# Two-layer hybrid encoder: token-on-partition projections in 512-column blocks, two token tiles at a time

## The chip, the cores and the metric

The kernel runs on one core of a Trainium2 chip. The metric is the device time of one execution in microseconds, as the median of a few runs. Everything is computed in fp32; large matmuls are done in three passes on operands that are split into two exact parts (called hi and lo below).

## What is computed

The reference is a trunk of two layers over 512 tokens of 1024 features. Each layer is a mixer and a convolutional FFN, each wrapped as x += RMSNorm(f(RMSNorm(x))).

```python
def _ssd_mlstm_mixer(h, w_in, ...):          # layer 0
    z, xbc, dt_raw, q, k, v, o_pre, gates = _split(h @ w_in, L0_SPLITS)
    xbc = jax.nn.silu(_dwconv(xbc, conv_w, conv_b))
...
    y = _head_rmsnorm(y.reshape(bsz, s, SSD_D_INNER) * jax.nn.silu(z), ssd_norm, SSD_GROUPS)
...
    hm = jax.nn.sigmoid(o_pre) * hm.reshape(bsz, s, MLSTM_D)
    hm = _head_rmsnorm(hm, mlstm_norm, MLSTM_HEADS)
    return jnp.concatenate([y, hm], axis=-1) @ w_out

def _gla_mixer(h, w_in, ...):                # layer 1
    q, k, v, r, g_lr = _split(h @ w_in, L1_SPLITS)
...
    o = _head_rmsnorm(o.reshape(bsz, s, GLA_DV), gla_norm, GLA_HEADS) * jax.nn.silu(r)
    return o @ w_out
```

The projections z, v, o_pre (layer 0) and v, r (layer 1), each 1024 columns wide, are wanted with tokens on the partitions. The others (k, q, xbc, the small gates, all of the FFN and the output projections) are wanted with features on the partitions.

## The kernel before

**Projections.** Work comes in two forms. A `Job` (line 259) is one 128-row tile of W^T h: eight k steps of three matmuls, 512 tokens wide, 24 matmuls into one PSUM bank, with the weight as the stationary operand. `nat_job` (line 344) is the other form, h^T W: 256 weight columns, for each of the four tiles of 128 tokens 24 matmuls that are 256 columns wide, with h as the stationary operand. In the profile's names a Job's matmul is `pj<-s,hi` and a nat_job's is `pj<-hi,s` or `pj<-lo,s`; all of them carry the line of a recording helper (L105), so the rows are told apart by tile names.

**PSUM.** The eight banks are split into tags (line 1356): `pj` has two, used by the streams' projections, `ps` and `pm` have three each, used by the scans. A nat_job takes one `pj` bank per token tile, so the two banks alternate: while one is filled, the other is read out by `post`, which runs on ScalarE. For z and r (lines 684 and 1123) `post` is silu in the form z(1 + tanh(z/2)): ScalarE reads the bank once with Identity and the token's scale into SBUF, then takes tanh from SBUF, and VectorE multiplies. For layer 0's v and o (lines 868 and 873) it is two reads of 128 columns each, into two heads; for layer 1's v one read. A Job's `post` starts with a VectorE read of the bank (`s<-pj,srow`).

**Weights.** They stream from HBM in 234 slabs of 1024 columns. `w_prep` (line 222) loads a slab, casts it to its hi part on ScalarE and takes the rest (lo) on VectorE. Five hi/lo buffers exist (`W_SPLIT`), and a slab is prepared four ahead of the one in use. A Job uses one slab, a nat_job two, for all four token tiles.

**Order.** The mixers weave generators by estimated engine time (`weave`, line 47). In layer 0 stream A is the projections, in the order p0 x0 z0 p1 x1 z1 p2 p3 (line 1341): a "p" is four Jobs (k, q) and two nat_jobs (v, o), an "x" is three or six Jobs, a "z" two nat_jobs; after them come eight Jobs of the first output projection. Stream B is the gate rows and the SSD scan, stream C the mLSTM heads. In layer 1 stream A is five Jobs and eight nat_jobs (four v, four r), and two streams run two GLA heads each; head n waits for the marks `v{n}` and `r{n}`. The framework then schedules by this order as priority and by its own estimate of when an instruction is ready; on the chip each engine runs its queue strictly in the order that came out. Work tiles of 512 columns get one of 64 slots, planned from the traced order; tiles of 256 columns come from a pool of six.

Of the kernel before, what the change touches and what calls it, by code (L numbers as in the profile page):

```python
# [30 lines left out]
# columns of the constant block  # L31
# [9 lines left out]
class _Balance:  # L41
    """Work issued so far to TensorE and VectorE, in ns, to weave two streams evenly."""
# [4 lines left out]
    def weave(self, streams, done):  # L47
        """streams: (generator, engine whose work it is paced by, total ns of that work, head start in ns).
        The stream least far along goes on, if what it needs is done."""
        st = [{"g": g, "e": e, "n": float(n), "t": -lead / float(n), "need": None} for g, e, n, lead in streams]  # L50
        while st:
            ok = [x for x in st if x["need"] is None or x["need"] in done]
            assert ok, [x["need"] for x in st]
            x = min(ok, key=lambda x: x["t"])
            t0 = getattr(self, x["e"])
            try:
                x["need"] = next(x["g"])
            except StopIteration:
                st.remove(x)
            x["t"] += (getattr(self, x["e"]) - t0) / x["n"]  # L60


class _Life:
    """First and last use of every work tile, in program order, and from that a slot for each."""
# [16 lines left out]
    def plan(self, slots):  # L81
        """The slot that has been free for longest."""
        until, res = [-1] * slots, []
        for a, z in zip(self.first, self.last):
            i = min(range(slots), key=lambda j: until[j])
            assert until[i] < a or until[i] < 0, "too few slots"
            until[i] = z + 1
            res.append(i)
        return res


class _Eng:
    """An engine that notes which tiles its instructions touch and how long they take."""
# [37 lines left out]
def kernel(ctx: ExitStack, tc: tile.TileContext, xin, wst, cst, dsk, gw2, out, life=None, plan=None):  # L131
# [104 lines left out]
    def w_take(n, width=P):  # L236
        """The next n tiles of `width` columns of the stream, as (hi, lo) pairs."""
        res = []
        for _ in range(n):
            c0 = wstate["unit"]  # L240
            i, o = divmod(c0, 1024)
            while len(wstate["ready"]) < i + 1 + W_AHEAD and wstate["next"] < NSLAB:
                w_prep()
            hi, lo = wstate["ready"][i]
            res.append((hi[:, o:o + width], lo[:, o:o + width]))
            wstate["unit"] += width
        return res

    def mm3(o, a, b, first, last):
        """o += a^T b with operands in two exact parts."""  # L250
        (ah, al), (bh, bl) = a, b
        PE.matmul(o, ah, bh, start=first, stop=False)
        PE.matmul(o, ah, bl, start=False, stop=False)
        PE.matmul(o, al, bh, start=False, stop=last)
# [4 lines left out]
    class Job:  # L259
        """One 128-row tile of W^T h."""  # L260
# [38 lines left out]
    def run_group(jobs, r, mid=None, serial=False):  # L299
        """Several jobs together, one k tile after the other (or one job after the other)."""  # L300
# [43 lines left out]
    def nat_job(h, post, hi=False):  # L344
        """256 columns of h^T W with tokens on the partitions."""
        w = w_take(KD, 256)
        for c in range(NCH):
            o = pj()
            for k in range(KD):
                hh, hl = h[k]  # L350
                tk = slice(c * P, (c + 1) * P)
                mm3(o[:, :256], (hh[:, tk], hl[:, tk]), w[k], k == 0, k == KD - 1)
            with hp(hi):
                post(o[:, :256], c)
            yield

# [4 lines left out]
    def col_sum(o, i, acc):  # L361
        """o[tok, 2i + t]: the sum of acc[:, tok] over the partitions, for two tiles of tokens."""
        for t in range(2):
            PE.matmul(o[:, 2 * i + t:2 * i + t + 1], acc[:, t * P:(t + 1) * P], ones[:, 0:1], start=True, stop=True)

    def rstd(v, rs):
        """rs = 1 / sqrt(v / D + eps) for columns v."""
        S.activation(rs, v, AF.Sqrt, bias=eps1, scale=1.0 / D)
        V.reciprocal(rs, rs)

    def spread(o, rs):
        """o[p, tok] = rs[tok] on every partition."""
# [3 lines left out]
    def split(xk, g, h, n, r):  # L376
        """The two exact parts of x * g (the norm's per-token factor is applied to the products)."""
# [6 lines left out]
    class Scale:  # L384
        """1 / rms of x for every token: as columns [tok, tile] and as a row on all partitions."""
# [29 lines left out]
    class Post:  # L415
        """x += f * g * rstd, fed with f one row tile and one token half at a time."""
# [27 lines left out]
        def finish(self, r, nxt=None):  # L444
            """nxt: (layer, which, h) of the norm that follows."""
# [13 lines left out]
    def conv(o, sc, wc, b, taps):  # L459
        """Depthwise convolution along the tokens of a PSUM tile, scaled by token, into SBUF."""  # L460
# [57 lines left out]
    def mixer0(h, x_again, sc, chain_of):  # L518
        done = set()
        # small block: dt and gates  # L520
# [37 lines left out]
        def gate_rows():  # L558
# [7 lines left out]
            V.tensor_tensor(u, u, d, ALU.mult)           # z = e / (2 + e)  # L566
# [6 lines left out]
            V.tensor_tensor(u, u, d, ALU.mult)           # log1p(exp(-|g|))  # L573
# [34 lines left out]
            # SSD rows  # L608
# [15 lines left out]
            # mLSTM rows  # L624
# [32 lines left out]
            # rows to DRAM for broadcasts over the partitions  # L657
# [9 lines left out]
            # columns: [tok, chunk, (quantity of the pair, direction), head]  # L667
# [13 lines left out]
        zt = [[None] * 2 for _ in range(NCH)]  # L681

        def z_proj(nb):
            def post_z(o, c):
                gg, hf = divmod(nb, 2)
                if hf == 0:
                    zt[c][gg] = st()
                zz = t256()
                S.activation(zz, o, AF.Identity, scale=sc.col[:, c:c + 1])
                th = t256()  # L690
                S.activation(th, zz, AF.Tanh, scale=0.5)
                V.scalar_tensor_tensor(zt[c][gg][:, hf * 256:(hf + 1) * 256], th, 1.0, zz, ALU.add, ALU.mult)
            yield from nat_job(h, post_z, False)

# [162 lines left out]
        hcol = small([P, 4], "hcol")  # L857
        V.tensor_scalar(hcol, sc.col, 0.5, None, ALU.mult)

        def pair(i):  # L860
# [7 lines left out]
            def post_v(o, c):  # L868
# [3 lines left out]

            def post_o(o, c):
                for e in range(2):
                    S.activation(ot[2 * i + e][:, c * P:(c + 1) * P], o[:, e * P:(e + 1) * P], AF.Tanh,
                                 scale=hcol[:, c:c + 1])
            yield from nat_job(h, post_v, False)
            yield from nat_job(h, post_o, False)
# [123 lines left out]
        def stream_a():  # L1002
            for what, i in A_ORDER:
# [5 lines left out]
                else:  # L1009
                    yield from z_proj(2 * int(i))  # L1010
                    yield from z_proj(2 * int(i) + 1)
# [31 lines left out]
    def mixer1(h, x_again, sc, chain_of):  # L1043
# [34 lines left out]
        def after(ins, first):  # L1078
            """Issue order only: groups activations by their function table."""
# [32 lines left out]
        def v_proj(nb):  # L1112
            def post_v(o, c, nb=nb):
                if nb % 2 == 0:
                    t = st()
                    vt[c][nb], vt[c][nb + 1] = t[:, :256], t[:, 256:]
                S.activation(vt[c][nb], o, AF.Identity, scale=sc.col[:, c:c + 1])
            yield from nat_job(h, post_v, True)
            done.add(f"v{nb}")

        rt = [[None] * 4 for _ in range(NCH)]
        def r_proj(nb):
            def post_r(o, c, nb=nb):
                if nb % 2 == 0:
                    t = st()
                    rt[c][nb], rt[c][nb + 1] = t[:, :256], t[:, 256:]
                zz = t256()
                S.activation(zz, o, AF.Identity, scale=sc.col[:, c:c + 1])
                th = t256()
                S.activation(th, zz, AF.Tanh, scale=0.5)  # L1130
                V.scalar_tensor_tensor(rt[c][nb], th, 1.0, zz, ALU.add, ALU.mult)
            yield from nat_job(h, post_r, False)
            done.add(f"r{nb}")
# [5 lines left out]
        def head(hd, ps):  # L1139
# [7 lines left out]
            for dd in range(2):  # L1147
# [3 lines left out]
                # first / second 64 tokens of a block in the order of the scan  # L1151
# [12 lines left out]
                # kc: keys of the first half to its end, of the second half as they are  # L1164
# [20 lines left out]
                # whole-block operands of the states  # L1185
# [62 lines left out]
        def stream_a():  # L1248
            yield from run_full(jobs[NFIRST:])
            done.add("kq")  # L1250
            for nb in range(4):
                yield from v_proj(nb)
            for nb in range(4):
# [28 lines left out]
    def load_first(r):  # L1282
        """Half the tokens of x, two row tiles to a tile."""
# [80 lines left out]
def _layout(a):  # L1364
    """Host-side layout: transposed activations, weights in the order of use, packed vectors."""
# [22 lines left out]
    def pair(i):  # L1388
        i2 = slice(i * 256, (i + 1) * 256)
        nb(k[:, i2], 128), nb(q[:, i2], 128), tblock(v[:, i2]), tblock(o[:, i2])  # L1390
    xb(XBC_ORDER[:NFIRST - 1])
    for what, i in A_ORDER:
# [4 lines left out]
        else:  # L1397
            nb(z[:, 512 * int(i):512 * int(i) + 512], 256)
# [15 lines left out]
    nb(k, 128), nb(q, 128), nb(v, 256), nb(r, 256)  # L1414
# [36 lines left out]
def build(new, arrays):  # L1451
    """The program: traced once to learn how long each tile is in use, then with a slot for each."""
# [26 lines left out]
```

## Time and profile before

| what | value |
|---|---|
| median of three runs | 1556.7 us (1555.45 to 1556.77) |
| profiled execution, first to last instruction (its span) | 1554.8 us |
| median less that span | 1.9 us |
| TensorE matmul busy | 1508.2 us, 97% |
| VectorE, ScalarE busy | 1032.1 us, 730.6 us |
| mean granted TensorE clock | 0.992 of full |

The profiled execution's own time is known only as its span; what lies around it is the difference to the median. A share of busy time is a mean over stages: the stretch from about 62 to 430 us is layer 0's mixer, 960 to 1118 us is layer 1's. Rows of a timeline give start and duration in us, in brackets the idle time of the engine before and what ended it.

### The profile page before, as it was taken

To read this page: it belongs to the slowest core of one execution; us is meant where nothing else is said; L and a number is where in the kernel's file an instruction comes from. 1 tells how busy PE (TensorE), PEld (TensorE's weight loads), DVE (VectorE), ACT (ScalarE), POOL (GpSimd) and SP (SyncE) were. 2 spreads that over 40 slices of the span, in tenths; PEclk is the share of its full clock that TensorE was granted. 3 is DMA by queue.
4 is the path that set the end of the run, shared out by engine and by line. 5 is a ranking of instruction groups with operands and counts; after the bars stand their busy time and mean duration, and the time that the engine had idled before them with its cause. 6 is when DMAs were issued, how large, how long until landed. Compare 5 with 4: busy or idle time off the path is not lost.

```text
span 1554.8 us, 22022 instructions
## 1 busy us (share of the span) xinstructions
PE 1508.2 (97%) x8616; PEld 1300.3 (84%) x8616; DVE 1032.1 (66%) x1703; ACT 730.6 (47%) x1332; POOL 142.8 (9%) x165
## 2 busy tenths in 40 slices
PE   7989999999999999999999999999999999999997
PEld 6879887888987988888888997898899888888887
DVE  6986789967754888623676378737537974267744
ACT  6445545744642664423444356436545543244432
POOL 5020321212100110000000030000003000000000
PEclk9999999999999999999999999999999999999999
DMA  5243243334322322222222132211131322222211
GB/s 186 96 156 96 82 129 102 102 114 140 131 91 79 112 86 104 95 95 95 95 95 99 69 123 103 74 56 55 65 125 69 109 95 95 95 95 95 95 69 54
DMA packets 67303, 152.46 MB, mean 98 GB/s; under 512 B 6256, under 2 KB 32896, under 8 KB 67200
## 3 DMA queue, kind: packets, MB, share of 16 engines
q1 hardware_dynamic: 61984, 145.77, 27.7%
q10 hardware_dynamic: 4752, 4.23, 0.9%
q8 instruction: 67, 1.10, 0.3%
q0 software_dynamic: 464, 1.06, 0.2%
q14 instruction: 36, 0.29, 0.1%
HBM read 146.42 MB, written 4.59 MB: 97 GB/s over the span
## 4 chain that ended last, share of the span: by engine, by line
PE 80%; DVE 11%; ACT 4%; DMA 3%; issue 2%; POOL 0%; SPq 0%; DVEq 0%; ACTq 0%; POOLq 0%
PE pj L105 31%; PE ps L105 25%; PE pm L105 24%; DVE s L105 8%; DMA s<-rowd 2%; ACT s L105 2%; DVE lo L105 2%; DVE t L105 1%; ACT hi L105 1%; ACT L105 0%; DVE pacc L105 0%; DMA raw<-in_w 0%; POOL s L105 0%; ACT msq L105 0%; DVE rd L105 0%
## 5 line engine op out<-in xcount | busy, mean ns | idle before, releaser
L105 DVE TENSOR_TENSOR lo<-raw,hi 128x1024 fp32r<-128x1024 f32 x234 | 291.4, 1249 | 220.5 <-ACT hi L105 220.3
L105 PE MATMUL pj<-s,hi 128*128 128x512 f32 (+1 forms) x1384 | 405.4, 376 | 5.2 <-ACT s L105 5.2
L105 ACT CAST hi<-raw 128x1024 fp32r<-128x1024 f32 x234 | 244.3, 1048 | 241.7 <-PE pj L105 107.7
L105 PE MATMUL pm<-s,hi 128*128 128x512 f32 (+1 forms) x1140 | 309.9, 357 | 8.4 <-ACT s L105 6.8
L105 PE MATMUL ps<-s,hi 128*128 128x512 f32 (+1 forms) x1140 | 307.3, 356 | 0.7 <-DVE t L105 0.7
L105 PEld LDWEIGHTS pj<-s,hi 128*128 128x128 f32 x1384 | 248.7, 189 | 54.6 <-ACT s L105 5.6
L105 PE MATMUL pj<-s,lo 128*128 128x512 f32 (+1 forms) x692 | 257.3, 372 | 0.0
L105 PE MATMUL pj<-hi,s 128*128 128x256 f32 x1280 | 241.6, 286 | 6.6 <-DVE s L105 3.0
L105 PEld LDWEIGHTS pm<-s,hi 128*128 128x128 f32 x1140 | 202.7, 190 | 41.6 <-ACT s L105 6.8
L105 PEld LDWEIGHTS ps<-s,hi 128*128 128x128 f32 x1140 | 202.2, 190 | 33.2 <-issue 1.1
L105 PEld LDWEIGHTS pj<-hi,s 128*128 128x128 f32 x1280 | 200.4, 189 | 9.1 <-DVE s L105 3.6
L105 PE MATMUL ps<-s,lo 128*128 128x512 f32 (+1 forms) x570 | 203.0, 356 | 1.2 <-DVE lo L105 1.2
L105 PE MATMUL pm<-s,lo 128*128 128x512 f32 (+1 forms) x570 | 203.1, 356 | 0.0
L105 PE MATMUL pj<-lo,s 128*128 128x256 f32 x640 | 180.7, 282 | 0.0
L105 DVE SCALAR_TENSOR_TENSOR s<-s,cc,s 128x511 f32<-128x511 f32 (+1 forms) x240 | 168.0, 712 | 3.2 <-ACT s L105 0.8
L105 ACT ACTIVATE s<-s 128x512 f32<-128x512 f32 (+1 forms) x145 | 90.3, 629 | 154.8 <-DVE s L105 137.0
L105 DVE TENSOR_TENSOR s<-s,s 128x512 f32<-128x512 f32 (+3 forms) x214 | 136.3, 651 | 34.0 <-ACT s L105 31.9
L105 PEld LDWEIGHTS pj<-s,lo 128*128 128x128 f32 x692 | 130.6, 189 | 23.8 <-issue 1.0
L105 ACT ACTIVATE s<-s,cc 128x512 f32<-128x512 f32 (+2 forms) x188 | 121.8, 664 | 38.2 <-DVE s L105 37.3
L105 PEld LDWEIGHTS ps<-s,lo 128*128 128x128 f32 x570 | 108.2, 190 | 17.6 <-DVE lo L105 1.6
L105 PEld LDWEIGHTS pj<-lo,s 128*128 128x128 f32 x640 | 121.5, 190 | 1.5 <-issue 1.0
L105 PEld LDWEIGHTS pm<-s,lo 128*128 128x128 f32 x570 | 108.3, 190 | 15.8
(155 smaller groups left out, 1342.5 us busy)
## 6 DMA issues: line engine op xcount, KB each, us to landing
raw<-in_w SPq DMA_DIRECT2D x234, 512.0 KB, 3.2
s<-rowd SPq DMA_DIRECT2D x64, 256.0 KB, 3.8
s<-in_x SPq DMA_DIRECT2D x8, 256.0 KB, 6.0
s<-in_x ACTq DMA_DIRECT2D x16, 128.0 KB, 2.7
xsave<-s SPq DMA_DIRECT2D x16, 128.0 KB, 2.3
s<-xsave ACTq DMA_DIRECT2D x16, 128.0 KB, 2.4
out_x<-s SPq DMA_DIRECT2D x16, 128.0 KB, 1.8
rowd<-s POOLq DMA_DIRECT2D x3, 128.0 KB, 2.3
```

The costliest lines, as they stand in the source:

```text
L105: return f(*a, **k)
```

## The change

A nat_job now takes 512 weight columns and works on two token tiles together: both `pj` banks are open, and for each k step three matmuls go into the first and three into the second. It yields to the other streams in the middle and at the end of each pair. The two `post` calls come after the pair. v and o of a head pair share one block (256 columns each), and the weight layout on the host follows. silu takes tanh first and Identity second, both by ScalarE from PSUM on 512 columns, and uses 512-column work tiles; the halved token scale `hcol` that tanh needs is computed earlier in layer 0 and anew in layer 1. The marks v0 and v1 (and so on in pairs) are set together.

```diff
     def nat_job(h, post, hi=False):
-        """256 columns of h^T W with tokens on the partitions."""
-        w = w_take(KD, 256)
-        for c in range(NCH):
-            o = pj()
+
+        w = w_take(KD, 512)
+        for c0 in range(0, NCH, 2):
+            os = [pj(), pj()]
             for k in range(KD):
                 hh, hl = h[k]
-                tk = slice(c * P, (c + 1) * P)
-                mm3(o[:, :256], (hh[:, tk], hl[:, tk]), w[k], k == 0, k == KD - 1)
-            with hp(hi):
-                post(o[:, :256], c)
+                for o, c in zip(os, (c0, c0 + 1)):
+                    tk = slice(c * P, (c + 1) * P)
+                    mm3(o, (hh[:, tk], hl[:, tk]), w[k], k == 0, k == KD - 1)
+                if k % QUANT == QUANT - 1 and k < KD - 1:
+                    yield
+            for o, c in zip(os, (c0, c0 + 1)):
+                with hp(hi):
+                    post(o, c)
             yield
+
+    def silu2_of(sc, hcol):
+
+        def f(o, c):
+            zz, th = st(), st()
+            S.activation(th, o, AF.Tanh, scale=hcol[:, c:c + 1])
+            S.activation(zz, o, AF.Identity, scale=sc.col[:, c:c + 1])
+            V.scalar_tensor_tensor(zz, th, 1.0, zz, ALU.add, ALU.mult)
+            return zz
+        return f
...
-        def z_proj(nb):
+        def z_proj(gg):
             def post_z(o, c):
-                gg, hf = divmod(nb, 2)
-                if hf == 0:
-                    zt[c][gg] = st()
-                zz = t256()
-                S.activation(zz, o, AF.Identity, scale=sc.col[:, c:c + 1])
-                th = t256()
-                S.activation(th, zz, AF.Tanh, scale=0.5)
-                V.scalar_tensor_tensor(zt[c][gg][:, hf * 256:(hf + 1) * 256], th, 1.0, zz, ALU.add, ALU.mult)
+                zt[c][gg] = silu2(o, c)
             yield from nat_job(h, post_z, False)
...
-            def post_v(o, c):
+            def post_vo(o, c):
                 for e in range(2):
                     S.activation(vx[2 * i + e][:, c, 0:P], o[:, e * P:(e + 1) * P], AF.Identity,
                                  scale=sc.col[:, c:c + 1])
-
-            def post_o(o, c):
                 for e in range(2):
-                    S.activation(ot[2 * i + e][:, c * P:(c + 1) * P], o[:, e * P:(e + 1) * P], AF.Tanh,
+                    S.activation(ot[2 * i + e][:, c * P:(c + 1) * P], o[:, 256 + e * P:256 + (e + 1) * P], AF.Tanh,
                                  scale=hcol[:, c:c + 1])
-            yield from nat_job(h, post_v, False)
-            yield from nat_job(h, post_o, False)
+            yield from nat_job(h, post_vo, False)
...
         def v_proj(nb):
-            def post_v(o, c, nb=nb):
-                if nb % 2 == 0:
-                    t = st()
-                    vt[c][nb], vt[c][nb + 1] = t[:, :256], t[:, 256:]
-                S.activation(vt[c][nb], o, AF.Identity, scale=sc.col[:, c:c + 1])
+            def post_v(o, c):
+                t = st()
+                vt[c][2 * nb], vt[c][2 * nb + 1] = t[:, :256], t[:, 256:]
+                S.activation(t, o, AF.Identity, scale=sc.col[:, c:c + 1])
             yield from nat_job(h, post_v, True)
-            done.add(f"v{nb}")
+            done.update((f"v{2 * nb}", f"v{2 * nb + 1}"))
...
+        hcol = small([P, 4], "hcol1")
+        V.tensor_scalar(hcol, sc.col, 0.5, None, ALU.mult)
+        silu2 = silu2_of(sc, hcol)
+
         def r_proj(nb):
...
-                zz = t256()
-                S.activation(zz, o, AF.Identity, scale=sc.col[:, c:c + 1])
-                th = t256()
-                S.activation(th, zz, AF.Tanh, scale=0.5)
-                V.scalar_tensor_tensor(rt[c][nb], th, 1.0, zz, ALU.add, ALU.mult)
+            def post_r(o, c):
+                t = silu2(o, c)
+                rt[c][2 * nb], rt[c][2 * nb + 1] = t[:, :256], t[:, 256:]
             yield from nat_job(h, post_r, False)
-            done.add(f"r{nb}")
+            done.update((f"r{2 * nb}", f"r{2 * nb + 1}"))
```

The number of slabs, the bank counts, the five split buffers and the weave's parameters stay as they are.

## Rows read from the trace of the kernel before

**Rows 1.** The page: busy time of each engine, share of the span, instructions.

```profile
PE 1508.2 (97%) x8616; PEld 1300.3 (84%) x8616; DVE 1032.1 (66%) x1703; ACT 730.6 (47%) x1332; POOL 142.8 (9%) x165
```

**Rows 2.** Windows: busy us (instructions) of PE, PEld, DVE, ACT, POOL; clock, DMA.

```profile
62.00:111.00 49.00, 45.13 (x293) 41.02 (x291) 43.37 (x62) 21.45 (x37) 8.75 (x9) 0.97 0.40 127
111.00:430.00 319.00, 307.72 (x2009) 271.26 (x2010) 253.36 (x489) 177.07 (x420) 65.78 (x55) 0.99 0.36 112
960.00:1118.00 158.00, 154.58 (x1114) 142.11 (x1114) 98.13 (x198) 85.02 (x166) 5.90 (x8) 1.00 0.17 58
```

**Rows 3.** Waits of the matmul queue, layer 0's mixer: total us, times, longest.

```profile
PE pj L105 <- ACT s L105: 5.2, 2, 3.5
...
PE pj L105 <- ACT t L105: 2.2, 1, 2.2
PE pj L105 <- DVE s L105: 1.3, 2, 1.1
```

**Rows 4.** The same view, layer 1's mixer.

```profile
PE pj L105 <- DVE s L105: 1.7, 1, 1.7
PE pj L105 <- ACT s L105: 1.4, 1, 1.4
```

**Rows 5.** Groups by shape, TensorE: busy us, mean ns, idle before.

```profile
L105 PE MATMUL pj<-hi,s 128*128 128x256 f32 x1280 | 241.6, 286 | 6.6 <-DVE s L105 3.0 <-ACT t L105 2.2 <-ACT s L105 1.4
```

**Rows 6.** Windows of TensorE alone: 256-column matmuls, then 512-column ones.

```profile
112.00:131.50 19.50, 19.50 (x166) 1.00 0.27 96
...
600.00:700.00 100.00, 100.00 (x433) 1.00 0.27 95
```

**Rows 7.** Timeline of VectorE at one entry: start us, us.

```profile
175.47 0.68 DVE L105 SCALAR_TENSOR_TENSOR s<-pj,srow 128x512 f32<-128x512 f32 x1
```

**Rows 8.** Timeline of TensorE at the same entry.

```profile
170.78 0.28 PE L105 MATMUL pj<-hi,s 128*128 128x256 f32 x1
```

**Rows 9.** Timeline of VectorE at the last entry.

```profile
973.72 0.68 DVE L105 SCALAR_TENSOR_TENSOR s<-pj,srow 128x512 f32<-128x512 f32 x1
```

**Rows 10.** Timeline of TensorE at the last entry.

```profile
969.77 0.28 PE L105 MATMUL pj<-hi,s 128*128 128x256 f32 x1
```

**Rows 11.** Groups by shape, ScalarE.

```profile
L105 ACT ACTIVATE t<-pj,scol 128x256 f32<-128x256 f32 x32 | 15.1, 470 | 26.5 <-PE pj L105 26.3
...
L105 ACT ACTIVATE t<-t 128x256 f32<-128x256 f32 x32 | 13.3, 416 | 0.6
```

**Rows 12.** Timeline of ScalarE: two reads of 512 PSUM columns in a row.

```profile
1083.75 1.25 ACT L105 ACTIVATE s<-pm,gnh 128x512 fp32r<-128x512 f32 x2
```

**Rows 13.** Timeline of ScalarE: the first read of the first tile.

```profile
65.90 0.37 ACT L105 ACTIVATE s<-pj,scol 128x128 f32<-128x128 f32 x1 [2.01 <-PE pj L105]
```

**Rows 14.** Timeline of ScalarE: the reads of the seventh tile.

```profile
88.65 0.62 ACT L105 ACTIVATE s<-pj,hcol 128x128 f32<-128x128 f32 x2
```

**Rows 15.** Timeline of TensorE around that read.

```profile
85.55 0.28 PE L105 MATMUL pj<-hi,s 128*128 128x256 f32 x1
89.33 0.73 PE L105 MATMUL pj<-s,hi 128*128 128x512 f32 x2 [3.50 <-ACT s L105]
```

**Rows 16.** Timeline of ScalarE inside one silu: a table load.

```profile
1109.68 1.28 ACT L105 ACT_TABLE_LOAD   x1
```

**Rows 17.** Groups by shape, VectorE: silu's product.

```profile
L105 DVE SCALAR_TENSOR_TENSOR s<-t,t 128x256 f32<-128x256 f32 x32 | 13.6, 426 | 15.8 <-ACT t L105 15.7
```

**Rows 18.** Windows of instructions on ps banks, layer 0's mixer.

```profile
62.00:430.00 368.00, 52.84 (x280) 36.75 (x280) 27.38 (x40) 14.29 (x26) 0.99 0.37 114
```

**Rows 19.** Windows of instructions on pm banks, layer 0's mixer.

```profile
62.00:430.00 368.00, 45.52 (x328) 41.03 (x328) 34.12 (x94) 11.17 (x34) 0.99 0.37 114
```

**Rows 20.** The chain that ended last, 111 to 520 us, by line.

```profile
by line: PE pj L105 42.6%; PE pm L105 12.1%; DVE s L105 10.6%; PE ps L105 8.9%; DMA s<-rowd 8.9%; ACT s L105 5.0%; issue 3.9%; ACT hi L105 1.7%; DVE lo L105 1.5%; POOL s L105 1.3%; ACT L105 0.9%; ACT msq L105 0.9%; DVE rd L105 0.8%; ACT mst
```

**Rows 21.** Timeline of ScalarE: the cast of a weight slab.

```profile
254.20 1.03 ACT L105 CAST hi<-raw 128x1024 fp32r<-128x1024 f32 x1
```

**Rows 22.** Timeline of VectorE: the rest of the same slab.

```profile
270.48 1.21 DVE L105 TENSOR_TENSOR lo<-raw,hi 128x1024 fp32r<-128x1024 f32 x1
```

More of the change, by code (lines that the diff above doesn't have):

```diff
@@ L678, in gate_rows @@
                     colq.append(tv)
+        hcol = small([P, 4], "hcol")
+        V.tensor_scalar(hcol, sc.col, 0.5, None, ALU.mult)
+        silu2 = silu2_of(sc, hcol)
         zt = [[None] * 2 for _ in range(NCH)]
-        def z_proj(nb):
+        def z_proj(gg):
             def post_z(o, c):
-                gg, hf = divmod(nb, 2)
-                if hf == 0:
-                    zt[c][gg] = st()
-                zz = t256()
-                S.activation(zz, o, AF.Identity, scale=sc.col[:, c:c + 1])
-                th = t256()
-                S.activation(th, zz, AF.Tanh, scale=0.5)
-                V.scalar_tensor_tensor(zt[c][gg][:, hf * 256:(hf + 1) * 256], th, 1.0, zz, ALU.add, ALU.mult)
+                zt[c][gg] = silu2(o, c)
             yield from nat_job(h, post_z, False)
@@ L856, in mixer0 @@
         vx, ot = [None] * 8, [None] * 8
-        hcol = small([P, 4], "hcol")
-        V.tensor_scalar(hcol, sc.col, 0.5, None, ALU.mult)
         def pair(i):
@@ L1009, in stream_a @@
                 else:
-                    yield from z_proj(2 * int(i))
-                    yield from z_proj(2 * int(i) + 1)
+                    yield from z_proj(int(i))
                     done.add("z" + i)
@@ L1112, in v_proj @@
         def v_proj(nb):
-            def post_v(o, c, nb=nb):
-                if nb % 2 == 0:
-                    t = st()
-                    vt[c][nb], vt[c][nb + 1] = t[:, :256], t[:, 256:]
-                S.activation(vt[c][nb], o, AF.Identity, scale=sc.col[:, c:c + 1])
+            def post_v(o, c):
+                t = st()
+                vt[c][2 * nb], vt[c][2 * nb + 1] = t[:, :256], t[:, 256:]
+                S.activation(t, o, AF.Identity, scale=sc.col[:, c:c + 1])
             yield from nat_job(h, post_v, True)
-            done.add(f"v{nb}")
+            done.update((f"v{2 * nb}", f"v{2 * nb + 1}"))
         rt = [[None] * 4 for _ in range(NCH)]
+        hcol = small([P, 4], "hcol1")
+        V.tensor_scalar(hcol, sc.col, 0.5, None, ALU.mult)
+        silu2 = silu2_of(sc, hcol)
         def r_proj(nb):
[L1123 to L1126, printed above, removed]
-                zz = t256()
-                S.activation(zz, o, AF.Identity, scale=sc.col[:, c:c + 1])
-                th = t256()
-                S.activation(th, zz, AF.Tanh, scale=0.5)
-                V.scalar_tensor_tensor(rt[c][nb], th, 1.0, zz, ALU.add, ALU.mult)
+            def post_r(o, c):
+                t = silu2(o, c)
+                rt[c][2 * nb], rt[c][2 * nb + 1] = t[:, :256], t[:, 256:]
             yield from nat_job(h, post_r, False)
-            done.add(f"r{nb}")
+            done.update((f"r{2 * nb}", f"r{2 * nb + 1}"))
         gnh = small([P, 8], "gnh")
@@ L1250, in stream_a @@
             done.add("kq")
-            for nb in range(4):
+            for nb in range(2):
                 yield from v_proj(nb)
-            for nb in range(4):
+            for nb in range(2):
                 yield from r_proj(nb)
@@ L1389, in pair @@
         i2 = slice(i * 256, (i + 1) * 256)
-        nb(k[:, i2], 128), nb(q[:, i2], 128), tblock(v[:, i2]), tblock(o[:, i2])
+        nb(k[:, i2], 128), nb(q[:, i2], 128), tblock(np.concatenate([v[:, i2], o[:, i2]], axis=1))
     xb(XBC_ORDER[:NFIRST - 1])
@@ L1397, in _layout @@
         else:
-            nb(z[:, 512 * int(i):512 * int(i) + 512], 256)
+            tblock(z[:, 512 * int(i):512 * int(i) + 512])
     wo = f("ab_w_out")[0]
@@ L1413, in _layout @@
     tblock(pad([(0, glr[:, :16]), (32, glr[:, 16:])]))
-    nb(k, 128), nb(q, 128), nb(v, 256), nb(r, 256)
+    nb(k, 128), nb(q, 128), nb(v, 512), nb(r, 512)
     nb(f("c_w_out")[0], 128)
```

## The prediction

> **What bounds the kernel now.** I read the page first: TensorE is busy 97% of the span [rows 1], so only what changes its queue counts: time per matmul, and time without one. Then the windows over the two stretches with the changed projections: TensorE is close to full in all three pieces, VectorE is at 253 of 319 us in the second [rows 2]; it is not the bound, but work queues on it. Then the matmul queue's waits for a `pj` bank: 8.7 us in layer 0's mixer [rows 3], 3.1 in layer 1's [rows 4], 11.8 together. Last the timelines around those waits, to see how soon after its last matmul a bank is free again. The reader is to see that today's waits are few because one bank is filled while the other is read.
>
> **What each matmul gives.** The nat_jobs issue 1280 matmuls with hi moving [rows 5] and half as many with lo: 20 nat_jobs x 4 tiles x 24 = 1920. After the change 10 x 4 x 24 = 960 of twice the width. In an unbroken stretch 166 of 256 columns start in 19.5 us, 117.5 ns each; 433 of 512 columns start in 100 us, 230.9 ns each [rows 6]. So a pair costs 235.0 today and 230.9 afterwards: 4.1 ns x 960 = **3.9 us saved**. That 960 weight loads go saves nothing more: the 512-column pitch already stands for one load per matmul, hidden.
>
> **What the two open banks cost.** Today a tile of 24 matmuls takes 24 x 0.1175 = 2.8 us, and that is the time its neighbour's bank has to be read out. Afterwards both banks fill together (48 x 0.231 = 11.1 us a pair), finish 3 x 0.231 = 0.69 us apart, and both are wanted again at once, 0.69 us apart. Three kinds of places:
>
> *Entry* (a nat_job behind a Job). The second bank is the one that the last Job just filled, and VectorE must read it. It is wanted 0.69 us after the start, where it used to be 2.8. I compared the end of VectorE's read with the start of the nat_job at all seven entries. The largest: 175.47 + 0.68 = 176.15 [rows 7] against 170.78 + 0.69 [rows 8], 4.7 us late. The last: 974.40 [rows 9] against 969.77 + 0.69 [rows 10], 3.9 us. The other five are 0.3, 3.4, 2.9, 2.4 and 2.4. Sum 20.0 us, before anything covers it.
>
> *Middle* (between the two pairs of one nat_job). With T the end of the pair, ScalarE starts on the first bank at T - 0.69. Today one silu of 256 columns is 470 + 416 ns [rows 11], and only the 470 hold the bank. Afterwards two reads of 512 columns do; the trace has no tanh of that shape, and the nearest rows are two scaled PSUM reads of 512 columns in a row, 1.25 us [rows 12]. The first bank is free at T + 0.6, the second, ScalarE being one queue, about 1.15 later at T + 1.75, wanted at T + 0.6 + 0.69. Wait: 0.6 + 0.5 = 1.1 us. v and o read four times 128 columns, two in 0.62 [rows 14], so the same. Layer 1's v reads once: about 0.
>
> *Exit* (a Job behind a nat_job): only the first bank is wanted, 0.6 us.
>
> To these comes ScalarE's own lateness. The first tile's read waits for TensorE and starts as the tile ends [rows 13], as do 23 of layer 0's 48 tiles; but 19 of the 48 start over 1 us late, since ScalarE's queue stands at something else: the seventh tile's reads start at 88.65 [rows 14], when TensorE had finished the tile behind it too and stood still [rows 15]. Over the timelines the mean is 1.28 us for layer 0's 48 tiles, 0.57 for layer 1's 32. Today 2.8 us of slack swallow nearly all of it.
>
> Layer 0 has six nat_jobs: 6 x (1.1 + 1.28) + 6 x (0.6 + 1.28) = 14.3 + 11.3. Layer 1 has two v and two r without a gap: four boundaries of v at 0.57, three of r at 1.1 + 0.57, 2.3 + 5.0. With the entries 20.0 + 25.6 + 7.3 = 52.9 us of bank waits, less the 11.8 paid today: **up to 41.1 us more**.
>
> At this place the Trainium skill speaks on both sides. "Perfetto Trace Analysis", section Optimizing Tensor Performance, says that independent matmul groups should rotate through different PSUM banks, so that the evacuation of one overlaps the matmuls of the next, and that larger matmuls are more efficient when possible. The trace agrees with the first where the banks rotate (read starts of layer 0's early tiles cost TensorE nothing), and with the second by the 4.1 ns above; by the second alone the sum would be -3.9, by the first alone up to +41.1.
>
> **How much of it lands.** A bank wait costs only if TensorE has nothing else in its queue. Streams B and C issue matmuls on `ps` and `pm`, busy 52.8 and 45.5 us in layer 0's mixer [rows 18, 19], and the order puts them at the places where stream A yields. But the queue's order is fixed beforehand: the lateness of ScalarE is not foreseen in it, and in the 3.5 us wait at 85.55 nothing else ran [rows 15]. On the other side a wait gives VectorE and ScalarE time to catch up, so the next is shorter; they do not simply add. Between nothing and all I take four tenths, nearer to nothing as the foreseen floors (1.1, 0.6) mostly lie where B and C have work: 16.4 us.
>
> **The rest, costed at nothing.** silu on ScalarE: 32 x (0.470 + 0.416) = 28.4 us become 16 x 1.25 = 20.0; VectorE's 32 products of 426 ns [rows 17] become 16 longer ones. Neither is the bound, TensorE covers it; without that cover it would be a gain of some 8 us. Where silu follows another function, a table load of 1.28 us stands between its two steps today, behind the bank's release [rows 16]; with tanh first it stands ahead of it. That happens once in 32: at most 1.3 us. `hcol` is one four-column instruction. Head 0 of layer 1 may start one nat_job later, 22.2 - 11.3 = 10.9 us; the cover is that VectorE is at 98 of 158 us there [rows 2] and that TensorE has the r projections meanwhile; if it is gone, up to 10.9 us.
>
> **Sum.** Against the profiled span 1554.8 (the median is 1.9 above it): 1554.8 - 3.9 + 16.4 + 1.9 = **1569.2 us**, 0.8% slower. Bounds: no wait lands and today's 11.8 go as well, 1541.0; all land, 1593.9.
>
> **Rivals.**
>
> 1. *Faster: the waits are filled.* If at each of the boundaries `ps` and `pm` matmuls stand ready, only the pitch counts: 1552.8 us, lower if today's waits are filled too. For it: 98 us of such work in layer 0's mixer, against 25.6 + (20.0 - 3.9) = 41.7 us of waits there without cover. Against it: in the first 50 us of that stretch the gate rows run on VectorE and the waits of today were not filled. It decides when less than 2% of the 41.1 lands (0.8 us).
>
> 2. *No change that can be measured.* Stream A is not always what sets the end: of the chain from 111 to 520 us `pj` matmuls are 42.6%, the rest goes through VectorE, ScalarE, `rowd` transfers and the scans' matmuls [rows 20]. A wait of stream A that falls where the scan is late anyway costs nothing. Between 2% and 17% landing (0.8 to 7.0 us) the time lies within 1553.6 to 1559.8.
>
> 3. *Much slower: weight slabs come late.* A nat_job holds four of five split buffers; the first comes free a quarter into the second pair, 11.1 + 2.8 = 13.9 us after the start, and the next nat_job wants the slab behind it at 22.2 + 2.8 = 25.0, 11.1 us later. Preparing a slab can take longer: one is cast at 254.20 [rows 21] and its rest ends at 270.48 + 1.21 [rows 22], 17.5 us. At layer 1's three joins this would cost up to 3 x 6.4 = 19 us on top: 1588. Against it: that lag lies in layer 0, where VectorE is fuller and Jobs follow, with 13.8 us and more of cover.
>
> **Chances.** Forecast 0.60 (a fifth to two thirds lands, 1561 to 1580), rival 1 0.20, rival 2 0.12, rival 3 0.08. Slower is the forecast and rival 3, 0.68. About 0.2% (3.1 us) is what a measurement of this kernel can tell from no change. The range for 8 in 10 takes in the better part of rival 1 and the forecast and ends where rival 3 begins: 1552 to 1588.
>
> **What would show it.** Right: the matmul queue's waits for `pj` (on ScalarE and VectorE) rise from 11.8 to some 28 us in the two stretches; 640 and 320 matmuls of 512 columns at a pitch near 231 ns; the FFN stretches unchanged; entries with the second bank wanted 0.69 us after the start. Wrong: those waits stay near 12 us, or `ps` and `pm` matmuls stand in them (rival 1); the waits rise but the mixers' ends do not move (rival 2); matmuls wait for `lo` or `hi` (rival 3). The step that is weakest is the share of four tenths.

## The result and the profile after

The changed kernel takes 1568.7 us (median of four, 1566.8 to 1570.2) against 1556.1 for the kernel before on the same chip: ratio 1.0083, 95% interval 1.0069 to 1.0097. The forecast was 1569, with a range of 1552 to 1588. The profiled execution spans 1565.1 us, 10.3 more than before; its own time, 1566.8 us, is the lowest of the four.

The page, busy time of each engine:

```profile
PE 1512.5 (97%) x7656; PEld 1255.6 (80%) x7656; DVE 1026.4 (66%) x1688; ACT 719.9 (46%) x1290; POOL 142.0 (9%) x165
```

There are 960 matmuls and weight loads fewer than in [rows 1], and TensorE's busy time is not smaller but 4.3 us larger. The other 6.0 of the span's 10.3 us are idle time (46.6 before, 52.6 after). The changed groups by shape, TensorE:

```profile
L105 PE MATMUL pj<-hi,s 128*128 128x512 f32 x640 | 214.8, 408 | 15.0 <-DVE s L105 11.0 <-ACT s L105 4.0
...
L105 PE MATMUL pj<-lo,s 128*128 128x512 f32 x320 | 128.8, 403 | 0.0
```

The matmul queue's waits for a `pj` bank (total us, times, longest) in layer 0's mixer, which answers to [rows 3]:

```profile
PE pj L105 <- ACT s L105: 8.8, 5, 3.9
PE pj L105 <- DVE s L105: 7.6, 3, 3.9
```

and in layer 1's mixer, which answers to [rows 4]:

```profile
PE pj L105 <- DVE s L105: 3.4, 1, 3.4
```

8.7 us have become 16.4 and 3.1 have become 3.4: 19.8 in place of 11.8. All that is new stands at entries: the waits for VectorE, which are the entries, grew from 3.0 to 11.0 us; those for ScalarE, which are the middles and exits, were 8.8 us and are 8.8 us. TensorE at the largest entry in layer 0, where a nat_job follows the q Jobs (start, duration, idle before):

```profile
170.88 0.39 PE L105 MATMUL pj<-hi,s 128*128 128x512 f32 x1
171.11 0.39 PE L105 MATMUL pj<-lo,s 128*128 128x512 f32 x1
171.35 0.63 PE L105 MATMUL pj<-hi,s 128*128 128x512 f32 x2
171.81 0.39 PE L105 MATMUL pj<-lo,s 128*128 128x512 f32 x1
176.06 0.79 PE L105 MATMUL pj<-hi,s 128*128 128x512 f32 x1 [3.86 <-DVE s L105]
```

and VectorE's read of the second bank there:

```profile
175.33 0.68 DVE L105 SCALAR_TENSOR_TENSOR s<-pj,srow 128x512 f32<-128x512 f32 x1
```

The matmuls start 0.23 us apart. Five of them stand ahead of the wait, not three: by the order of hi and lo on both sides of it, two belong to the first bank's next k step, put ahead by the framework (inferred, as the rows don't name the bank). So the second bank is wanted 1.16 us after the start, and is read out only at 175.33 + 0.68 = 176.01. TensorE goes on at 176.06. In [rows 7, 8] VectorE read the bank at nearly the same time, and nothing waited for it: 24 matmuls into the first bank came first, then a scan's, and one of these waited for an operand of its own until VectorE was done:

```profile
176.98 0.49 PE L105 MATMUL pm<-mst_c,s 128*128 128x129 f32 x2 [2.10 <-ACT mst_c L105]
```

That wait is gone after the change, so this place costs 3.86 - 2.10 us, about 1.8 more. The entry of layer 1's v, which answers to [rows 9, 10]:

```profile
980.05 0.40 PE L105 MATMUL pj<-hi,s 128*128 128x512 f32 x1
...
980.98 0.40 PE L105 MATMUL pj<-lo,s 128*128 128x512 f32 x1
984.74 0.80 PE L105 MATMUL pj<-hi,s 128*128 128x512 f32 x1 [3.37 <-DVE s L105]
```

Layer 1's v starts 10.3 us later than in [rows 10], and the span is 10.3 longer: all of the loss lies ahead of this point, and what layer 1 loses at this entry it gains back elsewhere. Of it, 9.0 us are lost by the time of the norm that closes layer 0's mixer (its first matmul starts at 549.61 us, before the change at 540.61).

Not every long wait is an entry. The middle of the second z block, TensorE and then ScalarE:

```profile
271.50 0.39 PE L105 MATMUL pj<-hi,s 128*128 128x512 f32 x1
274.67 0.80 PE L105 MATMUL pj<-hi,s 128*128 128x512 f32 x1 [2.78 <-ACT s L105]
```

```profile
273.39 0.66 ACT L105 ACTIVATE s<-pj,hcol 128x512 f32<-128x512 f32 x1
273.95 0.67 ACT L105 ACTIVATE s<-pj,scol 128x512 f32<-128x512 f32 x1
```

The first bank of the pair is read out at 274.62, as ScalarE came to it late. Before the change TensorE waited 2.2 us between two z blocks of 256 columns there, the `ACT t` row of [rows 3]. The two reads of 512 columns take 1.23 us in a row, forecast from [rows 12] at 1.25.

The last view answers to nothing in the prediction. The 10 us of TensorE from the end of each of the five long bank waits (us busy, matmuls, granted clock):

```profile
91.59:101.59 10.00, 10.00 (x33) 0.73 0.68 253
176.06:186.06 10.00, 9.99 (x51) 0.86 0.27 80
274.67:284.67 10.00, 10.00 (x41) 0.84 0.27 82
332.16:342.16 10.00, 10.00 (x43) 0.83 0.27 79
984.74:994.74 10.00, 10.00 (x37) 0.84 0.18 53
```

The same for the kernel before: behind its two long bank waits (89, 271), and at the three other places, where its waits are 2.1 us for a scan's tile (174), none (330) and 1.4 us (975):

```profile
89.33:99.33 10.00, 10.00 (x37) 0.83 0.71 198
174.00:184.00 10.00, 7.90 (x68) 1.00 0.46 124
271.15:281.15 10.00, 9.81 (x68) 0.83 0.30 107
330.00:340.00 10.00, 10.00 (x87) 1.00 0.24 80
975.00:985.00 10.00, 8.62 (x73) 1.00 0.15 54
```

A granted clock of 0.83 over 10 us is 1.7 us of full clock lost, 0.73 is 2.7. After: 2.7 + 1.4 + 1.6 + 1.7 + 1.6 = 9.0 us; before: 3.4 us. So behind these bank waits the clock was at its lower level (1.2 GHz) for part of the time that followed, and that is 5.6 us more than before, besides the waits' own length. There is one more such stretch, 1.7 us, behind a wait of 1.2 us that both kernels have, at that norm:

```profile
548.00:558.00 10.00, 8.80 (x60) 0.83 0.14 50
```

and before the change:

```profile
539.00:549.00 10.00, 8.79 (x73) 1.00 0.14 51
```

Whether the change has to do with that one is not shown.

### The profile page after: what moved, and what is told of

It reads as the page before. It is cut to its first block, busy times and chain, and to the rows that moved or that the text cites. A ratio compares the mean times of both kernels' runs of the same rounds, so it can differ in the third digit from the quotient of the medians.

```text
span 1565.1 us, 20032 instructions
## 1 busy us (share of the span) xinstructions
PE 1512.5 (97%) x7656; PEld 1255.6 (80%) x7656; DVE 1026.4 (66%) x1688; ACT 719.9 (46%) x1290; POOL 142.0 (9%) x165
## 4 chain that ended last, share of the span: by engine, by line
PE 83%; DVE 10%; DMA 3%; ACT 3%; issue 1%; POOL 0%; DVEq 0%; SPq 0%; ACTq 0%; POOLq 0%
PE pj L105 34%; PE ps L105 24%; PE pm L105 24%; DVE s L105 7%; DMA s<-rowd 2%; ACT s L105 2%; DVE lo L105 1%; DVE t L105 1%; DVE pacc L105 0%; DMA raw<-in_w 0%; ACT L105 0%; ACT hi L105 0%; POOL s L105 0%; DVE rd L105 0%; ACT msq L105 0%
## 5 line engine op out<-in xcount | busy, mean ns | idle before, releaser
L105 PE MATMUL pj<-s,lo 128*128 128x512 f32 (+1 forms) x692 | 257.7, 373 | 0.0
L105 PE MATMUL pj<-hi,s 128*128 128x512 f32 x640 | 214.8, 408 | 15.0 <-DVE s L105 11.0
L105 PEld LDWEIGHTS pj<-hi,s 128*128 128x128 f32 x640 | 122.7, 192 | 47.8 <-DVE s L105 13.0
L105 PE MATMUL pj<-lo,s 128*128 128x512 f32 x320 | 128.8, 403 | 0.0
L105 POOL TENSOR_TENSOR s<-s,s 128x512 f32<-128x512 f32 (+1 forms) x56 | 71.2, 1276 | 423.7 <-DVE s L105 270.9
```

The source lines that it names most:

```text
L105: return f(*a, **k)
```

## The experiments

All were timed against the kernel before on the same chip; ratios are to it, intervals are 95%.

**The same pairs, in halves.** Only the order of the matmuls in a pair is altered, so that the two banks start and finish 2.8 us apart:

```diff
-            for k in range(KD):
-                hh, hl = h[k]
-                for o, c in zip(os, (c0, c0 + 1)):
-                    tk = slice(c * P, (c + 1) * P)
-                    mm3(o, (hh[:, tk], hl[:, tk]), w[k], k == 0, k == KD - 1)
-                if k % QUANT == QUANT - 1 and k < KD - 1:
-                    yield
+            for kq in range(0, KD, QUANT):
+                for o, c in zip(os, (c0, c0 + 1)):
+                    tk = slice(c * P, (c + 1) * P)
+                    for k in range(kq, kq + QUANT):
+                        hh, hl = h[k]
+                        mm3(o, (hh[:, tk], hl[:, tk]), w[k], k == 0, k == KD - 1)
+                if kq + QUANT < KD:
+                    yield
```

> The changed kernel with only the order of matmuls inside a pair altered: the first bank takes k steps 0 to 3, then the second, then the first k 4 to 7, then the second. The same instructions, slabs, yields and readers. Now the banks start and finish 2.8 us apart instead of 0.69. Theory (the waits for the two banks that open and close together cost what the change lost): the entries shrink by 2.1 us each, the middles and exits vanish; of the 12 us lost at least 8 come back, 1553 to 1560 us. Rival 1 (the loss comes from the coarser order and yields, or from weight slabs held through two pairs): neither is altered, 1566 to 1571 us.

Measured: 1552.7 us, ratio 0.9985 (0.9972 to 0.9999). All of the loss has gone; the time lies just below the band. Its waits for `pj` in layer 0:

```profile
PE pj L105 <- ACT s L105: 5.3, 2, 3.4
...
PE pj L105 <- DVE s L105: 3.9, 3, 2.5
```

Entries still wait some, as VectorE is later than the 2.8 us that this order gives. The mean granted clock is 0.992, as before the change (0.987 after it).

**Pairs alone, 256 columns wide.** The kernel before, with two token tiles to a pair and the yields that go with it:

```diff
-        for c in range(NCH):
-            o = pj()
+        for c0 in range(0, NCH, 2):
+            os = [pj(), pj()]
             for k in range(KD):
...
-                mm3(o[:, :256], (hh[:, tk], hl[:, tk]), w[k], k == 0, k == KD - 1)
+                for o, c in zip(os, (c0, c0 + 1)):
+                    tk = slice(c * P, (c + 1) * P)
+                    mm3(o[:, :256], (hh[:, tk], hl[:, tk]), w[k], k == 0, k == KD - 1)
+                if k % QUANT == QUANT - 1 and k < KD - 1:
+                    yield
...
```

> The kernel before with one part of the change alone: nat_job stays 256 columns wide with its old readers and slabs, but works on two token tiles together, both banks open, a yield in the middle and after each pair. Theory (the open pair costs): entries as in the changed kernel, twice as many middles and exits, no gain in pitch, so slower than before by as much as the change or more: 1565 to 1585 us. Rival (512 columns, their slabs held or the longer readers cost): within 3 us of before, 1553 to 1560 us.

Measured: 1579.6 us, ratio 1.0153 (1.0138 to 1.0168). The open pair alone costs more than the whole change; as the first experiment keeps the yields and loses nothing, they are not the cause. Waits in layer 0, then the first and last of seven 10-us windows behind long waits (six for a `pj` bank, one for a scan's tile), all seven with the same granted clock:

```profile
PE pj L105 <- DVE s L105: 8.6, 4, 4.0
PE pj L105 <- ACT s L105: 7.7, 4, 3.1
PE pj L105 <- ACT t L105: 4.8, 1, 4.8
```

```profile
92.00:102.00 10.00, 8.99 (x32) 0.83 0.82 267
...
993.00:1003.00 10.00, 7.61 (x51) 0.83 0.16 59
```

**silu's double read alone.** The kernel before, with tanh and Identity both from the 256-column bank (for z and for r alike, with `hcol` computed as in the change):

```diff
-                zz = t256()
-                S.activation(zz, o, AF.Identity, scale=sc.col[:, c:c + 1])
-                th = t256()
-                S.activation(th, zz, AF.Tanh, scale=0.5)
+                zz, th = t256(), t256()
+                S.activation(th, o, AF.Tanh, scale=hcol[:, c:c + 1])
+                S.activation(zz, o, AF.Identity, scale=sc.col[:, c:c + 1])
```

> The kernel before with the other part alone: silu of z and r reads its 256-column bank twice on ScalarE (tanh with the halved scale, then Identity). Theory: the bank is held 0.9 us instead of 0.47, inside the 2.8 us that the other bank takes to fill, so no change: 1553.5 to 1559 us. Rival (the second PSUM read is what the change pays): 1562 us or more.

Measured: 1556.0 us, ratio 1.0000 (0.9989 to 1.0011). It costs nothing where the banks alternate.

**The changed kernel with the old silu.**

```diff
-            S.activation(th, o, AF.Tanh, scale=hcol[:, c:c + 1])
             S.activation(zz, o, AF.Identity, scale=sc.col[:, c:c + 1])
+            S.activation(th, zz, AF.Tanh, scale=0.5)
```

> The changed kernel with silu as before (Identity from the bank, tanh from SBUF), 512 columns wide. Theory: a bank of z and r is freed 0.6 us earlier, at two middles and two exits in layer 0 and three boundaries in layer 1; at most 7 x 0.6 to 1.1 us, of which under half lands: 1564 to 1569 us. Rival (the double read is the main loss): 1560 us or less.

Measured: 1568.4 us, ratio 1.0081 (1.0066 to 1.0096), as the change itself. A bank of z or r freed earlier at a middle or exit is worth nothing here; those of v and o were not altered.

**Entries alone.** In the changed kernel the last Job ahead of each nat_job takes a `ps` bank, so both `pj` banks are free at an entry:

```diff
-... [Job(h, post=post_cp(qT, 2 * i + e, 1.0)) for e in range(2)]
+... [Job(h, post=post_cp(qT, 2 * i + e, 1.0), psum=ps if e else pj) for e in range(2)]
-... psum=pa if n < NFIRST - 1 else pj)
+... psum=pa if n < NFIRST - 1 else ps if n in (5, 11) else pj)
-... [Job(h, post=post_cp(qT, i, P ** -0.5), hi=True) for i in range(4)]
+... [Job(h, post=post_cp(qT, i, P ** -0.5), psum=ps if i == 3 else pj, hi=True) for i in range(4)]
```

> The changed kernel, except that the last Job ahead of each nat_job in the streams (the second q Job of a pair, the last xbc Job of each group, layer 1's last q Job) accumulates in a ps bank in place of a pj bank, so both pj banks are long read out at an entry. The pairs stay as they are. In the changed kernel's trace five entries of this kind hold TensorE for 1.8 to 4.0 us, 14.5 in all. If the entries are the main part of what the waits cost: 1556 to 1563 us. If the middles and exits are: 1565 us or more. If the entries are paid by other streams anyway: unchanged, 1567 to 1570.

Measured: 1560.7 us, ratio 1.0024 (1.0007 to 1.0041): 1.0083 - 1.0024 = 0.59%, some 9 of the 12.6 us, come back. The waits for `pj` in layer 0, where none for VectorE is left, then in layer 1:

```profile
PE pj L105 <- ACT s L105: 5.0, 5, 1.6
```

```profile
PE pj L105 <- ACT s L105: 3.5, 1, 3.5
```

All entry waits are gone, 11.0 us. The expectation counted five and 14.5 us, but one of them, the 2.8 us at 272, is the middle shown above. Part of the time reappears elsewhere: layer 1's 3.5 us now stand in the middle of v's first block, and in layer 0 matmuls on `ps` banks wait for VectorE, which they hardly did in the change (0.4 us):

```profile
PE ps L105 <- DVE s L105: 4.0, 4, 2.1
```

**Halves in the first pair only, and in the second pair only.** The edit of the first experiment, under `if c0 == 0` and under `if c0 > 0`.

> The changed kernel with the first pair of each nat_job in halves (first bank k 0 to 3, second bank k 0 to 3, and so on) and the second pair as in the change. Entries ask for the second bank 2.1 us later; the first pair's banks finish 2.8 us apart, so the middle goes too; exits stay. Main part entries and middles: 1553 to 1560 us. Main part exits: 1564 us or more.

> The changed kernel with the second pair of each nat_job in halves and the first as in the change. Entries stay; a middle keeps its wait for the first bank (0.6 us and ScalarE's lateness) and loses that for the second; exits go. Main part entries: 1563 to 1569 us. Main part middles and exits: 1560 us or less.

Measured: first pair 1563.9 us, ratio 1.0043 (1.0026 to 1.0060); second pair 1571.0, ratio 1.0092 (1.0075 to 1.0109). The first falls between its two bands, at the very edge of the one for exits: VectorE's waits shrink, but those for ScalarE grow. 9.5 of their 13.0 us stand at exits, where a Job waits behind the second pair (5.3, 3.4 and 0.9 us; 4.9 together in the change). The first pair's waits in layer 0:

```profile
PE pj L105 <- ACT s L105: 13.0, 6, 5.3
PE pj L105 <- DVE s L105: 4.3, 3, 2.2
```

The second, in the same view, keeps the entries as they are, gains nothing, and lies 2 us above its band for entries:

```profile
PE pj L105 <- ACT s L105: 8.4, 4, 4.2
PE pj L105 <- DVE s L105: 8.1, 3, 3.8
```

The two do not add up to the halves in both pairs, which bring back some 15 us: a wait removed at one place can come up at the next.

**One token tile at a time, 512 columns.**

```diff
-        for c0 in range(0, NCH, 2):
-            os = [pj(), pj()]
...
+        for c in range(NCH):
+            o = pj()
+            tk = slice(c * P, (c + 1) * P)
+            for k in range(KD):
+                hh, hl = h[k]
+                mm3(o, (hh[:, tk], hl[:, tk]), w[k], k == 0, k == KD - 1)
+            with hp(hi):
+                post(o, c)
+            yield
```

> The changed kernel with one token tile at a time on 512 columns: 24 matmuls into one bank, post, a yield, then the next tile in the other bank. The slabs are held longest here: the first of the four comes free only in the fourth tile, so the next nat_job's slabs have 5.5 us less to be prepared. Theory (open pairs cost, slabs do not): no entry, middle or exit waits, pitch gain kept: 1550 to 1556 us. Rival (slabs held for long cost): 1560 us or more, with matmuls waiting for hi or lo.

Measured: 1549.8 us, ratio 0.9961 (0.9946 to 0.9977), faster than before and a little below the band. Its waits for `pj` in layer 0:

```profile
PE pj L105 <- ACT s L105: 2.0, 2, 1.1
...
PE pj L105 <- DVE s L105: 0.5, 1, 0.5
```

In layer 1 one wait of 0.3 us for a slab's lo is left. Holding four slabs through all four tiles costs nothing that can be seen.

**The entry edit on three other kernels**: as a control on the kernel before, on one tile at a time, and on the halves.

> Control for the entries: the kernel before with the last Job ahead of each nat_job in a ps bank. Before, the second bank is wanted 2.8 us after an entry, and two entries wait 1.15 and 1.7 us. Theory: at most these 2.9 us come back, 1553 to 1556 us, so the 9 us that the same edit gave the changed kernel belong to the open pairs. Rival (ps banks for these Jobs help by themselves, by order): 1550 us or less.

> One token tile at a time on 512 columns (the fastest so far) with the last Job ahead of each nat_job in a ps bank. There the second bank is wanted 5.5 us after an entry, so nothing waits at entries: theory 1548 to 1552 us, no change from one tile at a time alone.

> The changed kernel in halves, with the last Job ahead of each nat_job in a ps bank: both kinds of wait gone. Theory: the halves' remaining entry waits (2.6, 2.0, 1.3, 0.4 and 1.9 us in its trace) go as well, of which under half lands: 1548 to 1552 us.

Measured: before with the edit 1557.7 us, ratio 1.0009 (1.0000 to 1.0018): no gain, above its band (its two entry waits are gone, but one of 3.3 us stands in layer 1's v and 3.1 us of waits on `ps` have come up); one tile at a time with it 1549.6, 0.9959 (0.9943 to 0.9976), unchanged; halves with it **1545.5 us, 0.9932** (0.9919 to 0.9944), the fastest of all, faster than both kernels and 2.5 us below its band. The page of the last:

```profile
span 1545.8 us, 20034 instructions
...
PE 1503.5 (97%) x7656; PEld 1251.2 (81%) x7656; DVE 1028.6 (67%) x1688; ACT 720.8 (47%) x1290; POOL 145.6 (9%) x165
```

and its waits for `pj` in layer 0:

```profile
PE pj L105 <- ACT s L105: 3.4, 1, 3.4
```

## Why the prediction was right

**The pitch (-3.9 us).** Confirmed in the rows, 0.23 us between matmuls of 512 columns. The halves with free entries have TensorE busy for 1503.5 us, 4.7 less than [rows 1], at the same mean granted clock of 0.992.

**The entries (20.0 us before any cover).** The step that carried the result. VectorE is late as forecast at six of the seven: counted from 0.69 us after the start, 0.3, 4.4, 3.3, 2.4, 2.5 and 4.0 us (forecast 0.3, 4.7, 2.9, 2.4, 2.4, 3.9). At the second, forecast at 3.4, it is 0.2: TensorE gets there 3.2 us later, VectorE at the same time, as the prediction says of waits that shorten the next. TensorE waits at four, 3.9, 2.1, 1.7 and 3.4 us, 11.0 together against 3.0 before; at the fourth entry (257.7) matmuls of the scan and of the first bank filled the time. The entry edit gives back 9 us of the change and nothing of the kernel before.

**The middles and exits (32.9 us before any cover).** Mis-sized: they land at nothing on balance, 8.8 us of waits for ScalarE before and 8.8 after. The largest are old ones, the 3.9 us of [rows 15]'s place and the 2.8 at the middle of the second z block (2.2 before). The old silu and the halves in the second pair alone bring nothing back. That work of B and C at the yields covers the rest is the likely reason; it was not tested by itself.

**The share of four tenths (16.4 us).** Too high as a count of bank waits: 8.0 us landed, and the prediction's some 28 us of waits are 19.8. A scan's wait went away in exchange, so TensorE's idle time rose by 6.0. What made up the rest was not in the sum, the lower clock. The changed kernel is busy for 1512.5 us at a mean granted clock of 0.987, the halves with free entries for 1503.5 with as many matmuls at 0.992: 9.0 us, of which 5.6 lie behind the long bank waits and 1.7 behind the norm; the rest was not traced. So busy time is up by 9.0 - 4.7 = 4.3 us and idle time by 6.0, the 10.3 of the span. That the total came out right is luck: one term was too large by about what the other lacked.

**The rest at nothing.** Confirmed for silu's second read (1.0000). For layer 1's marks there is only the balance: layer 1 as a whole loses nothing behind the start of v. Layer 0's FFN, forecast as unchanged, takes 1.3 us more, no more than the lower clock at its start costs.

**Rivals.** The waits were not filled at the entries but for one, so the first rival failed on its place, though its size is what the kernels without these waits show. The second failed: the wait of stream A did move the mixer's end, by some 9 us. The third failed: the kernel that holds the slabs longest is faster than before. Why the halves with free entries end 4 us below one tile at a time with free entries, when both have few waits for `pj` left, stays open; their intervals just touch.

## What to carry to other kernels

Opening two accumulation banks together takes away the time in which one is read while the other fills, and here the price was paid where the bank comes from another reader: compare, at each such entry, the moment the second bank is wanted with the end of its reader in the trace. Wider matmuls were worth only their pitch (4 ns a pair here); with the banks staggered, by the order of the k steps or by taking one tile at a time, the same width turned from 0.8% slower to 0.15 to 0.4% faster, and to 0.7% with the halves and free banks at the entries. Freeing a bank earlier at the middles and exits brought nothing here. A wait of two to four microseconds can cost more than its length, in the clock of what follows. And name the place of each wait before adding it up: the 2.8 us at 272 look like an entry by their length, and are a middle where the kernel before waited 2.2.

## What the runs showed of the hardware

In the changed kernel TensorE's granted clock was 0.83 to 0.86 over the 10 us behind four bank waits of 2.1 to 3.9 us, and 0.73 behind a fifth, of 3.85 us, that ends at 91.59: that is partly at 1.2 instead of 2.4 GHz. The length of the wait does not settle it. In the kernel before it was 1.00 at the places with no wait (330), with one of 1.4 us (975) and with one of 2.1 us (174), but 0.83 behind one of 2.2 us (271). Behind the 1.2 us at the norm it was 0.83 in one kernel and 1.00 in the other. And in the halves it was 1.00 behind a bank wait of 3.4 us that ends at 88.54:

```profile
88.54:98.54 10.00, 10.00 (x43) 1.00 0.89 276
```

These are single profiled executions. The mean clock says the same of all: 0.986 to 0.987 in the four executions of the changed kernel, 0.992 on average in the 50 of the kernel before that the experiments took (0.985 to 0.995). With the pairs of 256 columns seven stretches at 0.83 stand in the mixers.
